# The T5 bias table laid out by the host and loaded in two pieces, and other dummy matmuls ahead of the first product

## The chip, the cores and the metric

One core of one Trainium2 chip runs the whole program. The metric is the device time of one execution in microseconds. The kernel before took 1897.99 us, the median of 3 runs (1896.04 to 1899.41).

## The reference, cut to what matters

Two transformer layers (`first_block`), then a layer with two other attentions and a product-key expert network (`second_block`), all in float32 for 256 tokens of width 1024. What the change touches is the bias of the sliding-window attention in the first two layers: a table of 32 buckets and 16 heads, spread over the distance between query and key. It is the same in both layers.

```
def sliding_window_attention(q, k, v, sinks, rel_bias):
    ...
    dist = np.arange(W)[:, None] + W - np.arange(2 * W)[None, :]
    bias = rel_bias.astype(jnp.float32)[t5_bucket(dist)]
    bias = bias.transpose(2, 0, 1).reshape(A_KV_HEADS, A_GROUP, W, 2 * W)
    valid_rel = jnp.asarray((dist >= 0) & (dist < W))
    ...
    logits = jnp.where(valid[None, :, None, None], scores + bias, -jnp.inf)
```

With W = 128, the table that the scores need has 128 queries x 16 heads x 256 keys: 2 MB in float32, with -1e30 outside the window.

## The kernel before, in words

**The products.** Nearly all of the work is matrix products of the activations with weights, each done as three float32r matmuls (`three`, lines 431 to 434; `prod_m`, lines 499 to 501), because a float32 operand is split into a high and a low part. The weights stream from HBM through the class `Weights`: `load` puts a block of 1 MB into one of three buffers (`raw`) from the SyncE queue, `first` makes the high part of half a block on ScalarE (line 264, six buffers `whi`), `second` the low part on VectorE (line 273, five buffers `wlo`). When both halves of a block are split, its buffer is free, and `second` issues the load of the block three further on. `pump` keeps the splitting four halves ahead of the half that is used. Blocks are numbered here from 0 in the order of `plan()`, halves likewise: block 8 is halves 16 and 17.

**The order.** `tc.manual_schedule()` keeps every engine's instructions in the order in which the Python code emits them, and every queue issues its DMAs in that order. Attention and other small work is woven between the products: generators stand in three lanes, and `tick()`, called at fixed places of a product, advances lane 0 or 1 at a rate, and lane 2 at `clock[4]`, which is 1.0 here, so one step of lane 2 for each tick. In `prod_t` with 8 input tiles each output block j has four ticks: after k = 3 and k = 7 of its first half, after k = 3 of its second, and at its end.

**The start.** The first block and the input come in pieces on the SyncE queue. Until they are there, five float32 matmuls on a tile of ones (`warm`, lines 356 and 357) keep TensorE at work. Their result is not used.

**The bias table.** `bias_load` (line 642) runs before the first layer: it takes the two tiles `BT[0]` and `BT[1]` (8 heads each, 1 MB each), loads the bucket table `rb` and the one-hot rows `oh`. `bias_table` (line 650) is put into lane 2 ahead of the product `aq` of layer 0 (line 791). It lets 15 ticks go by (`BW`), and at the 16th a matmul makes a row of 384 biases for each head (line 653), VectorE masks it (line 654), a DMA on GpSimd's queue writes 32 copies of it to DRAM (`toep`, line 658), and 8 more (line 663) read it back with a step of 383, so that each partition gets the row shifted by one.

**Who reads it.** `soft_pair` (line 699) does two heads. Its scores come from TensorE (lines 679 and 681), VectorE adds the bias of `BT[j // 4]` and takes the maximum (line 707), ScalarE the exponentials (line 714), VectorE scales them (lines 720 to 724), TensorE transposes them (line 729, six transposes for a pair), ScalarE copies them back (line 732), TensorE multiplies by the values (lines 690 and 692). In both layers the first pair's scores stand inside the first output block of the product `mqk`, the first six transposes follow the end of its second output block, then come four small transposes of the gates (lines 844 and 845), twelve product matmuls, and the next six transposes.

Of the kernel before, what the change touches and what calls it, by code (L numbers as in the profile page):

```python
# [9 lines left out]
F32 = mybir.dt.float32  # L10
F32R = mybir.dt.float32r
# [7 lines left out]
T = 256  # L19
KT = 8  # L20
EPS = 1e-6
NEG = -1e30
BW = 15
PR = (1.25, 1.65, 1.6, 1.5)
PZ = 2
GI = 3
LOOK, LAG, HI, LO, RAW = 4, 1, 6, 5, 3
FIRST, PIECE = 4, 512
NC = 32
NS, NA, NX, NB = 52, 60, 84, 96  # L30
KB = 0.61
GS = 2.0 ** 15
# [13 lines left out]
C_TRI = 256  # L46
C_CM = 384
C_ZM = 640
C_OH = 1024
C_ON = 1408  # L50
C_N = 1792

Q_HEADS = [(j, 4 + j) if j < 4 else (4 + j, 8 + j) for j in range(8)]

# [54 lines left out]
def lay_out(inp):  # L109

    f = {k: np.asarray(v) for k, v in inp.items()}
    offs = dict(mqk=0, mv=1024, mo=2048, gates=3072, aq=3080, ak=4104, av=4360, ga=4616, gb=5640)
    offs2 = dict(qa=0, ka=512, va=1024, qb=1536, kb=2048, vb=2560, g2a=3072, g2b=4096)
    hq = [h for pr in Q_HEADS for h in pr]
    aqcols = np.concatenate([np.arange(h * 64, h * 64 + 64) for h in hq])

    def tk(w, j):
        k = w.shape[0] // 128
        n = 16 // k
        b = w[:, j * n * 128:(j + 1) * n * 128].reshape(k, 128, n, 128)  # L120
        return b.transpose(1, 2, 0, 3).reshape(128, 2048)

    def mk(w, c0, nc, k0):
        nk = 2048 // nc
        b = w[k0 * 128:(k0 + nk) * 128, c0:c0 + nc].reshape(nk, 128, nc)
        return b.transpose(1, 0, 2).reshape(128, 2048)

    order = plan()
    wst = np.empty((len(order), 128, 2048), np.float32)
# [3 lines left out]
    for i, (nm, l, j) in enumerate(order):  # L133
        if nm == "aq":
            b = tk(waq[l], j)
        elif nm in ("ak", "mqk", "ga", "gb"):
            b = tk(f["w_in"][l][:, offs[nm]:offs[nm] + 1024], j)
        elif nm == "av":
            b = mk(f["w_in"][l], offs[nm], 256, 0)
        elif nm in ("mv", "mo"):  # L140
            b = mk(f["w_in"][l], offs[nm] + 512 * j[0], 512, 4 * j[1])
        elif nm == "ba":
            b = tk(wba[l], j)
        elif nm == "bm":
            b = tk(f["w_branch_m"][l], j)
        elif nm == "wo":
            b = tk(f["w_out"][l], j)
        elif nm == "up":
            b = tk(f["w_up"][l], j)
        elif nm == "dn":  # L150
            b = mk(f["w_down"][l], 0, 1024, 2 * j)
        elif nm in ("qa", "ka", "qb", "kb", "g2a", "g2b"):
            b = tk(f["w_in_2"][0][:, offs2[nm]:offs2[nm] + 1024], j)
        elif nm in ("va", "vb"):
            b = mk(f["w_in_2"][0], offs2[nm], 512, 4 * j)
        elif nm == "om":
            b = tk(f["w_out_moba_2"][0], j)
        elif nm == "os":
            b = tk(f["w_out_sb_2"][0], j)
        elif nm == "mix":  # L160
            b = tk(f["w_mix_out_2"][0], j)
        elif nm == "wq":
            b = tk(f["peer_w_q_2"][0], j)
        elif nm == "u":
            b = u[j * 256:(j + 1) * 256].reshape(2, 128, 8, 128).transpose(3, 0, 2, 1).reshape(128, 2048)
        elif nm == "v":
            b = v[j * 256:(j + 1) * 256].reshape(2, 128, 1024).transpose(1, 0, 2).reshape(128, 2048)
# [11 lines left out]
    for l in range(2):  # L179
# [9 lines left out]
    ii, jj = np.arange(128)[:, None], np.arange(128)[None, :]  # L189
    cst = np.zeros((128, C_N), np.float32)  # L190
    cst[:, C_ID:C_ID + 128] = np.eye(128)
# [3 lines left out]
    cst[:, C_ZM:C_ZM + 128] = strict  # L195
    cst[:, C_ZM + 256:C_ZM + 384] = strict
    cst[:, C_IO:C_IO + 128] = jj
    dist = 255 - np.arange(384)
    ok = (dist >= 0) & (dist < 128)
    n = np.maximum(dist, 0)  # L200
    large = 16 + (np.log(np.maximum(n, 1) / 16) / np.log(128 / 16) * 16).astype(np.int32)
    bucket = np.where(n < 16, n, np.minimum(large, 31))
    oh = (np.arange(32)[:, None] == bucket[None, :]) & ok[None, :]
    cst[:32, C_OH:C_OH + 384] = oh
    cst[:16, C_ON:C_ON + 384] = np.where(ok, 0.0, NEG)[None]

    q = np.arange(128)[:, None]
    c = np.arange(256)[None, :]
    dd = (128 + q - c).astype(np.float32)
    slopes = np.exp2(-np.arange(1, 9, dtype=np.float32))  # L210
    ali = np.where(dd >= 0, -slopes[:, None, None] * dd, np.float32(NEG)).astype(np.float32)
# [9 lines left out]
        "mg": np.ascontiguousarray(f["mlstm_norm_g"]),  # L221
        "fg": np.ascontiguousarray(f["final_norm_g_2"].reshape(1, D)),
        "sk": np.ascontiguousarray(f["peer_sub_keys_2"].reshape(16, 128, 128).transpose(2, 0, 1).reshape(128, 2048)),
        "rb": np.ascontiguousarray(f["rel_bias"][:, hq]),
    }


# [74 lines left out]
        return r  # L302


def body(tc, wst, xt, pk_d, cst_d, alibi_d, mg_d, fg_d, sk_d, rb_d, out):
    nc = tc.nc

    with tc.tile_pool(name="main", bufs=1) as sp, tc.tile_pool(name="wk", bufs=1) as wk, \
            tc.tile_pool(name="ws", bufs=1) as wp, tc.tile_pool(name="ps", bufs=1, space=PSUM) as ps, \
            tc.tile_pool(name="dr", bufs=1, space=bass.MemoryType.DRAM) as dr, tc.manual_schedule():  # L310
        pools = {}

        def slot(tag, dt=F32, n=2048):
            return pools["at"].tile([128, n], dt, name=tag, tag=tag)

        ws = Weights(nc, wp, wst, plan())
        mm, act, dve = nc.tensor.matmul, nc.scalar.activation, nc.vector

        def bank(tag, n):
            return ps.tile([128, 512], F32, name=tag, tag=tag, bufs=n)  # L320
# [7 lines left out]
        def sdb():  # L328
            return bank("sd", 1)

        def v3(t, a, b, off=0):
            return t[:, off:off + a * b].rearrange("p (a b) -> p a b", a=a)
# [13 lines left out]
        cst = wk.tile([128, 256], F32, name="cst")  # L346
# [6 lines left out]
        ones = wk.tile([128, 256], F32, name="ones")  # L353
        dve.memset(ones, 1.0)
        warm = sdb()
        for _ in range(5):
            mm(warm[:, :T], ones[:, :128], ones, start=True, stop=True)
        mhalf = wk.tile([128, 2], F32, name="mhalf")
        dve.memset(mhalf, -0.5)


        lanes = [deque(), deque(), deque()]
# [41 lines left out]
        def idle(n):  # L404
            for _ in range(n):
                yield
# [121 lines left out]
        def gain(i):  # L528
            return pk[:, PK_G + 8 * i:PK_G + 8 * i + 8]
# [20 lines left out]
        def norm_pair(j, g):  # L550
            for k in (2 * j, 2 * j + 1):
                act(H[0][:, k], X[:, k], AF.Identity, scale=g[:, k:k + 1])  # L552
            for k in (2 * j, 2 * j + 1):
                dve.scalar_tensor_tensor(H[1][:, k], X[:, k], g[:, k:k + 1], H[0][:, k].bitcast(F32),  # L554
                                         op0=OP.mult, op1=OP.subtract)
# [3 lines left out]
        def norm_sums(*later, now=True, ahead=LOOK):  # L559

            if ahead is not None:
                ws.pump(ws.used + 2 + ahead)
            later = list(later)
            if now:
                for _ in sum_sq(acc):
                    pass
            else:
                later[:0] = [(acc, None)]
            sums[:] = [sum_sq(a, g) for a, g in later]
            lanes[2].extend(sums)  # L570
# [68 lines left out]

        BT = []  # L640

        def bias_load():
            BT.extend(v3(slot(f"BT{i}"), 8, T) for i in range(2))
            rb = wk.tile([32, 16], F32, name="rb")
            nc.sync.dma_start(rb, rb_d)
            oh, row = [pools["at"].tile([128, 768], F32, name="oh", tag="L", bufs=2) for _ in range(2)]
            nc.sync.dma_start(oh, cst_d[:, C_OH:])
            return rb, oh, row[:16, :384]

        def bias_table(rb, oh, row):  # L650
            yield from idle(BW)
            p = sdb()
            mm(p[:16, :384], rb, oh[:32, :384], start=True, stop=True)
            dve.tensor_add(row, p[:16, :384], oh[:16, 384:])

            n = NC
            d = dr.tile([16, n, 384], F32, name="toep")
            nc.gpsimd.dma_start(d, row[:, None, :].to_broadcast([16, n, 384]))
            for i in range(2):
                for a in range(0, 128, n):  # L660
                    src = bass.AP(tensor=d.tensor, offset=d.offset + 8 * i * n * 384 + 127 - a,
                                  ap=[[383, n], [n * 384, 8], [1, 256]])
                    nc.gpsimd.dma_start(BT[i][a:a + n], src)
            yield


        OW = ((0, 128), (128, 256))
# [102 lines left out]
        def mixer(l):  # L770
# [11 lines left out]
                                             ap=[[0, 128], [1, D]]))  # L782
            wg = [pools["at"].tile([128, 160], F32R, name=n, tag="hm", bufs=2) for n in ("wgh", "wgl")]

            def ev_scaled(dst, r):
                def f(j, p):
                    dve.tensor_tensor(dst[:, 2 * j:2 * j + 2], v3(p, 2, T), b2(r), op=OP.mult)
                return f

            if l == 0:  # L790
                lanes[2].append(bias_table(*bias))
            prod_t("aq", H, ev_scaled(AQ, Rb8), 4, outer=(0,) if l else (), mid=mean_r if l else mean_0)
            parts(wg[0], wg[1], pk[:, PK_WG + 160 * l:PK_WG + 160 * l + 160])
            prod_t("ak", H, ev_scaled(AK, Rb), 1)
# [12 lines left out]
            for i in range(2):  # L807
                q = slice(32 * i, 32 * i + 4)
                dve.tensor_tensor(G[:, i], pg[q, :T], Rb[q], op=OP.mult)
                c = PK_BG + 2 * l + i  # L810
# [40 lines left out]
            c = PK_SK + 16 * l  # L851
# [575 lines left out]
        with tc.tile_pool(name="at", bufs=1) as pools["at"]:  # L1427
            ws.first()
            ws.second()
            for j in range(4):  # L1430
                norm_pair(j, gain(0))
            for _ in range(2):
                ws.first()
                ws.second()
            norm_sums(ahead=None)
            ws.pump(6)
            dve.tensor_mul(gff, gain(6), gain(4))
            bias = bias_load()
            pools["cst"] = pools["at"].tile([128, C_OH - 256], F32, name="catt")
            nc.sync.dma_start(pools["cst"], cst_d[:, 256:C_OH])  # L1440
            mixer(0)
            mlp(gain(2))
            mixer(1)
            acc2 = slot("BT1", n=512)
            mlp(gff, gain(6), acc2)
            mixer2(acc2)
# [23 lines left out]
```

## Time and profile before

| | |
|---|---|
| median of 3 runs | 1897.99 us |
| the profiled execution | 1896.21 us |
| its span, first to last instruction | 1894.4 us |
| mean granted clock of TensorE | 0.997 |
| DMA | 333.97 MB, 176 GB/s on the mean |

The profile is of one execution of its own, which lies 1.78 us under the median. 1.81 us of its time lie outside the span. Times in the rows are microseconds from the start of the span. A page of the profile gives totals; the views below are asked of the trace: who waited for whom, the instructions in order of time with the idle time ahead of each and what ended it, the chain of work that ended last, and sums by stretch.

### The profile page before, as it was taken

How to read it: one execution, taken by the hardware profiler on the slowest of the kernel's cores; microseconds unless marked ns; L12 is line 12 of the kernel's file. 1: busy time of each engine (PE TensorE's matmuls, PEld its weight loads, DVE VectorE, ACT ScalarE, POOL GpSimd, SP SyncE). 2: the span in 40 equal slices, each digit the busy share in tenths (PEclk: the TensorE clock that was granted, in tenths of full speed). 3: DMA queues.
4: the chain of work that ended last, by engine and by line, in shares of the span. 5: the costliest groups of instructions: out<-in, count | busy, mean ns of one | idle time of the engine just before them, and what ended most of it. 6: DMA issues, size and time to landing. Idle time of an engine off the chain costs nothing.

```text
span 1894.4 us, 34668 instructions
## 1 busy us (share of the span) xinstructions
PE 1878.1 (99%) x14450; PEld 1747.1 (92%) x14450; DVE 1351.8 (71%) x2426; ACT 977.5 (52%) x1441; POOL 28.0 (1%) x40
## 2 busy tenths in 40 slices
PE   9899999999999999999999999999999999999998
PEld 8779999999979999999989999999998888777786
DVE  5666666556686675556767799867988787888754
ACT  5476445445577455445555554644344444545443
POOL 0000000000000000000000000000000000000000
PEclk9999999999999999999999999999999999999999
DMA  8554445554344446454534545554445444555452
GB/s 287 166 178 145 160 181 206 182 196 165 148 161 163 156 179 222 178 184 162 189 134 162 217 163 197 191 185 156 157 159 188 167 179 178 200 189 178 165 194 87
DMA packets 48620, 333.97 MB, mean 176 GB/s; under 512 B 5656, under 2 KB 5920, under 8 KB 9552
## 3 DMA queue, kind: packets, MB, share of 16 engines
q1 hardware_dynamic: 46128, 322.29, 47.3%
q0 software_dynamic: 2048, 9.18, 1.8%
q8 instruction: 113, 1.85, 0.4%
q14 instruction: 43, 0.35, 0.1%
q10 hardware_dynamic: 288, 0.29, 0.0%
HBM read 328.85 MB, written 2.89 MB: 175 GB/s over the span
## 4 chain that ended last, share of the span: by engine, by line
PE 96%; DMA 2%; DVE 2%; ACT 0%; issue 0%; POOL 0%; SPq 0%; POOLq 0%; DVEq 0%; ACTq 0%
PE mm L432 17%; PE mm L433 17%; PE mm L434 17%; PE ac L1339 6%; PE ac L1341 6%; PE ac L1340 6%; PE ac L432 4%; PE ac L434 4%; PE ac L433 4%; PE mm L499 2%; PE mm L501 2%; PE mm L500 2%; PE sd L1277 1%; PE ac L1277 1%; PE ac L729 1%; PE ac L690 1%
## 5 line engine op out<-in xcount | busy, mean ns | idle before, releaser
L273 DVE TENSOR_TENSOR wlo<-raw,whi 128x1024 fp32r<-128x1024 f32 (+1 forms) x612 | 734.0, 1212 | 122.8 <-PE mm L434 61.9
L264 ACT CAST whi<-raw 128x1024 fp32r<-128x1024 f32 (+1 forms) x612 | 627.4, 1042 | 250.8 <-PE mm L433 128.6
L432 PE MATMUL mm<-Hh,whi 128*128 128x256 f32 x2288 | 654.7, 286 | 0.9 <-ACT Hh L552 0.9
L433 PE MATMUL mm<-Hl,whi 128*128 128x256 f32 x2288 | 645.0, 282 | 0.5 <-DVE Hl L554 0.3
L434 PE MATMUL mm<-Hh,wlo 128*128 128x256 f32 x2288 | 644.9, 282 | 0.2 <-DVE wlo L273 0.2
L432 PEld LDWEIGHTS mm<-Hh,whi 128*128 128x128 f32 x2288 | 431.7, 189 | 9.2 <-issue 5.8
L433 PEld LDWEIGHTS mm<-Hl,whi 128*128 128x128 f32 x2288 | 431.7, 189 | 1.7 <-DVE Hl L554 0.9
L434 PEld LDWEIGHTS mm<-Hh,wlo 128*128 128x128 f32 x2288 | 431.4, 189 | 0.4 <-DVE wlo L273 0.4
L1339 PE MATMUL ac<-whi,wvh 128*128 128x512 f32 x512 | 206.5, 403 | 0.0
L1341 PE MATMUL ac<-whi,wvl 128*128 128x512 f32 x512 | 202.9, 396 | 0.0
L1340 PE MATMUL ac<-wlo,wvh 128*128 128x512 f32 x512 | 201.9, 394 | 0.0
L432 PE MATMUL ac<-CV,whi 128*128 128x256 f32 x512 | 143.8, 281 | 0.0
L434 PE MATMUL ac<-CV,wlo 128*128 128x256 f32 x512 | 143.5, 280 | 0.0
L433 PE MATMUL ac<-MQ,whi 128*128 128x256 f32 x512 | 143.3, 280 | 0.0
L1341 PEld LDWEIGHTS ac<-whi,wvl 128*128 128x128 f32 x512 | 96.2, 188 | 22.8
L1340 PEld LDWEIGHTS ac<-wlo,wvh 128*128 128x128 f32 x512 | 96.5, 188 | 21.3
L1339 PEld LDWEIGHTS ac<-whi,wvh 128*128 128x128 f32 x512 | 96.4, 188 | 19.6
L1265 ACT COPY gs<-sd 128x252 f32<-128x252 f32 (+2 forms) x69 | 25.5, 370 | 153.1 <-PE sd L1277 153.1
L434 PEld LDWEIGHTS ac<-CV,wlo 128*128 128x128 f32 x512 | 96.7, 189 | 0.0
L433 PEld LDWEIGHTS ac<-MQ,whi 128*128 128x128 f32 x512 | 96.2, 188 | 0.0
L432 PEld LDWEIGHTS ac<-CV,whi 128*128 128x128 f32 x512 | 96.2, 188 | 0.0
L513 DVE TENSOR_TENSOR wvl<-A,wvh 128x512 fp32r<-128x512 f32 x58 | 40.0, 690 | 53.0 <-ACT wvh L512 47.7
(330 smaller groups left out, 2718.5 us busy)
## 6 DMA issues: line engine op xcount, KB each, us to landing
raw<-in_wst_dram SPq DMA_DIRECT2D x300, 1024.0 KB, 4.8
raw<-in_wst_dram SPq DMA_DIRECT2D x8, 512.0 KB, 7.7
BT<-toep POOLq DMA_DIRECT2D x8, 256.0 KB, 13.1
X<-in_xt_dram SPq DMA_DIRECT2D x4, 256.0 KB, 6.0
KV<-nMd POOLq DMA_DIRECT2D x2, 512.0 KB, 4.0
BT<-in_alibi_dram POOLq DMA_DIRECT2D x1, 1024.0 KB, 6.8
A<-in_sk_dram POOLq DMA_DIRECT2D x1, 1024.0 KB, 6.8
xs<-X POOLq DMA_DIRECT2D x1, 1024.0 KB, 10.1
```

What stands on the lines that cost most here:

```text
L264: self.nc.scalar.copy(hi[:, s], self.raw[p][:, h * 1024:(h + 1) * 1024][:, s])
L273: self.nc.vector.tensor_sub(lo[:, s], self.raw[p][:, h * 1024:(h + 1) * 1024][:, s], hi[:, s].bitcast(F32))
L432: mm(out_ap, hi, ah, start=first, stop=False, skip_group_check=True)
L433: mm(out_ap, hi, al, start=False, stop=False, skip_group_check=True)
L434: mm(out_ap, lo, ah, start=False, stop=last, skip_group_check=True)
L499: mm(o, a, hi[:, s], start=k == 0, stop=False)
L500: mm(o, a, lo[:, s], start=False, stop=False)
L501: mm(o, b, hi[:, s], start=False, stop=k == KT - 1)
L513: dve.tensor_sub(lo, src, hi.bitcast(F32))
L1339: mm(banks[i], a, hi, start=first, stop=False)
L1340: mm(banks[i], a, lo, start=False, stop=False)
L1341: mm(banks[i], c, hi, start=False, stop=last)
```

## The change

The host lays out the whole table (`bt`, 128 x 4096), and `bias_table` becomes two loads of 1 MB on the SyncE queue, straight into `BT[0]` and `BT[1]`: the first after 8 ticks of lane 2, the second after 4 more. `bias_load` goes, with its two loads, and with it go the matmul, the masking and the nine DMAs on GpSimd's queue. At the start four of the five float32 dummies stay, and nine float32r ones of 128, 64 and 96 columns follow, on a tile of ones that VectorE sets.

```diff
-BW = 15
+BW = 8, 4
...
+    bt = np.where(inside[:, :, None], f["rel_bias"][:, hq][bucket], np.float32(NEG)).transpose(0, 2, 1)
...
         warm = sdb()
-        for _ in range(5):
+        onesr = wk.tile([128, 512], F32R, name="onesr", tag="sq", bufs=2)[:, :128]
+        dve.memset(onesr.bitcast(F32), 1.0)
+        for _ in range(4):
             mm(warm[:, :T], ones[:, :128], ones, start=True, stop=True)
+        for n in (128, 128, 128, 64, 64, 64, 96, 96, 96):
+            mm(warm[:, :n], onesr, onesr[:, :n], start=True, stop=True)
...
-        def bias_load():
-            BT.extend(v3(slot(f"BT{i}"), 8, T) for i in range(2))
-            rb = wk.tile([32, 16], F32, name="rb")
-            nc.sync.dma_start(rb, rb_d)
-            oh, row = [pools["at"].tile([128, 768], F32, name="oh", tag="L", bufs=2) for _ in range(2)]
-            nc.sync.dma_start(oh, cst_d[:, C_OH:])
-            return rb, oh, row[:16, :384]
-
-        def bias_table(rb, oh, row):
-            yield from idle(BW)
-            p = sdb()
-            mm(p[:16, :384], rb, oh[:32, :384], start=True, stop=True)
-            dve.tensor_add(row, p[:16, :384], oh[:16, 384:])
-
-            n = NC
-            d = dr.tile([16, n, 384], F32, name="toep")
-            nc.gpsimd.dma_start(d, row[:, None, :].to_broadcast([16, n, 384]))
+        def bias_table():
+
             for i in range(2):
-                for a in range(0, 128, n):
-                    src = bass.AP(tensor=d.tensor, offset=d.offset + 8 * i * n * 384 + 127 - a,
-                                  ap=[[383, n], [n * 384, 8], [1, 256]])
-                    nc.gpsimd.dma_start(BT[i][a:a + n], src)
-            yield
+                yield from idle(BW[i])
+                nc.sync.dma_start(BT[i], bt_d[:, 2048 * i:2048 * i + 2048].rearrange("p (a b) -> p a b", a=8))
+                yield
...
-            bias = bias_load()
-            pools["cst"] = pools["at"].tile([128, C_OH - 256], F32, name="catt")
-            nc.sync.dma_start(pools["cst"], cst_d[:, 256:C_OH])
+            BT.extend(v3(slot(f"BT{i}"), 8, T) for i in range(2))
+            pools["cst"] = pools["at"].tile([128, C_N - 256], F32, name="catt")
+            nc.sync.dma_start(pools["cst"], cst_d[:, 256:])
```

## Rows read from the trace of the kernel before

**Rows 1.** The page: busy time, share of the span and instructions of each engine.

```profile
PE 1878.1 (99%) x14450; PEld 1747.1 (92%) x14450; DVE 1351.8 (71%) x2426; ACT 977.5 (52%) x1441; POOL 28.0 (1%) x40
```

**Rows 2.** Waits of TensorE, whole span: us in total, times, longest.

```profile
PE ac L729 <- DVE L L724: 4.5, 1, 4.5
...
PE mm L432 <- ACT Hh L552: 0.9, 1, 0.9
...
PE mm L434 <- DVE wlo L273: 0.2, 1, 0.2
```

**Rows 3.** The chain that ended last, 32 to 60 us: start, us, what.

```profile
34.51 9.55 DMA toep<-oh
...
46.14 12.00 DMA BT<-toep
```

**Rows 4.** Timeline of VectorE, layer 0: start, us, instruction, idle before and its releaser.

```profile
51.07 1.21 DVE L273 TENSOR_TENSOR wlo<-raw,whi 128x1024 fp32r<-128x1024 f32 x1
58.31 0.35 DVE L707 CUSTOM_DVE_ANT_0 L<-ac,BT,pk 128x128 f32<-128x128 f32 x1 [6.03 <-DMA BT<-toep]
...
66.81 1.03 DVE L724 TENSOR_TENSOR L<-L,sm 128x256 f32<-128x256 f32 x2
```

**Rows 5.** Timeline of TensorE, layer 0, first scores to the products after the transposes.

```profile
49.38 0.49 PE L679 MATMUL ac<-KV,AQ 64*128 64x128 f32 x4
...
62.65 0.28 PE L434 MATMUL mm<-Hh,wlo 128*128 128x256 f32 x1
67.38 0.30 PE L729 MATMUL ac<-cst,L 128*128 128x128 f32 x1 [4.45 <-DVE L L724]
67.98 1.30 PE L729 MATMUL ac<-cst,L 128*128 128x128 f32 x5 [0.30 <-DVE sm L720]
...
74.62 0.30 PE L432 MATMUL mm<-Hh,whi 128*128 128x256 f32 x1
```

**Rows 6.** Timeline of TensorE, the same places in layer 1.

```profile
491.29 0.49 PE L679 MATMUL ac<-KV,AQ 64*128 64x128 f32 x4
...
504.69 0.82 PE L729 MATMUL ac<-cst,L 128*128 128x128 f32 x6
...
508.39 0.28 PE L432 MATMUL mm<-Hh,whi 128*128 128x256 f32 x1
```

**Rows 7.** Timeline of VectorE, layer 1: the first pair's last step.

```profile
502.64 1.03 DVE L724 TENSOR_TENSOR L<-L,sm 128x256 f32<-128x256 f32 x2
```

**Rows 8.** Sums by stretch: busy us of each engine, granted clock, DMA share, GB/s.

```profile
66.00:70.00 4.00, 2.23 (x11) 1.67 (x11) 3.86 (x12) 1.19 (x3) 0.53 (x1) 0.73 0.41 171
70.00:75.00 5.00, 5.00 (x25) 5.00 (x25) 3.85 (x6) 3.08 (x7) 0.00 (x0) 0.54 0.60 213
...
504.00:508.00 4.00, 4.00 (x37) 3.81 (x35) 3.72 (x9) 0.63 (x3) 0.56 (x1) 1.00 0.11 17
```

**Rows 9.** Timeline of TensorE around the table's matmul of line 653.

```profile
32.59 0.28 PE L434 MATMUL ac<-Hh,wlo 128*128 128x256 f32 x1
...
33.54 0.39 PE L432 MATMUL mm<-Hh,whi 128*128 128x256 f32 x1
```

**Rows 10.** The SyncE queue: issues of weight blocks 5 to 7, 8 and 10.

```profile
21.37 8.22 SPq L241 DMA_DIRECT2D raw<-in_wst_dram  x3
36.22 0.33 SPq L241 DMA_DIRECT2D raw<-in_wst_dram  x1
...
50.83 0.33 SPq L241 DMA_DIRECT2D raw<-in_wst_dram  x1
```

**Rows 11.** Timeline of ScalarE: splits that waited for blocks 5, 6 and 8 to land.

```profile
29.55 2.00 ACT L264 CAST whi<-raw 128x1024 fp32r<-128x1024 f32 x2 [2.20 <-DMA raw<-in_wst_dram]
...
32.02 1.99 ACT L264 CAST whi<-raw 128x1024 fp32r<-128x1024 f32 x2 [0.25 <-DMA raw<-in_wst_dram]
...
47.82 1.05 ACT L264 CAST whi<-raw 128x1024 fp32r<-128x1024 f32 x1 [0.81 <-DMA raw<-in_wst_dram]
```

**Rows 12.** Timeline of TensorE: the dummy matmuls at the start.

```profile
1.19 4.63 PE L357 MATMUL sd<-ones 128*128 128x256 f32 x10 [1.19 <-DVE mhalf L359]
```

More of the change, by code (lines that the diff above doesn't have):

```diff
@@ L28 @@
 FIRST, PIECE = 4, 512
-NC = 32
 NS, NA, NX, NB = 52, 60, 84, 96
@@ L48 @@
 C_ZM = 640
-C_OH = 1024
-C_ON = 1408
-C_N = 1792
+C_N = 1024
 Q_HEADS = [(j, 4 + j) if j < 4 else (4 + j, 8 + j) for j in range(8)]
@@ L197, in lay_out @@
     cst[:, C_IO:C_IO + 128] = jj
-    dist = 255 - np.arange(384)
-    ok = (dist >= 0) & (dist < 128)
+    q = np.arange(128)[:, None]
+    c = np.arange(256)[None, :]
+    dist = 128 + q - c
     n = np.maximum(dist, 0)
@@ L202, in lay_out @@
     bucket = np.where(n < 16, n, np.minimum(large, 31))
[L203 to L208, printed above, removed]
+    inside = (dist >= 0) & (dist < 128)
+    bt = np.where(inside[:, :, None], f["rel_bias"][:, hq][bucket], np.float32(NEG)).transpose(0, 2, 1)
     dd = (128 + q - c).astype(np.float32)
@@ L223, in lay_out @@
         "sk": np.ascontiguousarray(f["peer_sub_keys_2"].reshape(16, 128, 128).transpose(2, 0, 1).reshape(128, 2048)),
-        "rb": np.ascontiguousarray(f["rel_bias"][:, hq]),
+        "bt": np.ascontiguousarray(bt.reshape(128, 4096)),
     }
@@ L302, in get_all, with body @@
         return r
-def body(tc, wst, xt, pk_d, cst_d, alibi_d, mg_d, fg_d, sk_d, rb_d, out):
+def body(tc, wst, xt, pk_d, cst_d, alibi_d, mg_d, fg_d, sk_d, bt_d, out):
     nc = tc.nc
@@ L790, in mixer @@
             if l == 0:
-                lanes[2].append(bias_table(*bias))
+                lanes[2].append(bias_table())
             prod_t("aq", H, ev_scaled(AQ, Rb8), 4, outer=(0,) if l else (), mid=mean_r if l else mean_0)
```

## The prediction

> **What bounds the kernel now.** The page comes first: TensorE is busy for 1878.1 us, 99% of the span [rows 1], so an edit counts only by what it takes from TensorE's stream or from TensorE's waits. The list of those waits comes second, because it is short: the longest is one wait of 4.5 us for VectorE's line 724, more than all the others together, and the next are 0.9 and 0.2 us at the start [rows 2]. So the third question is why line 724 was late. VectorE's timeline answers it: after the split that ends at 51.07 + 1.21 = 52.28 VectorE does nothing for 6.03 us, until the bias table has landed [rows 4]. The chain of waits shows where the table was: 9.55 us in the write to DRAM, then 12.00 us in the strided read back [rows 3]. Fourth, TensorE's timeline: it runs on with products until 62.65 + 0.28 = 62.93, then has nothing that it may do for 4.45 us, and once more for 0.30 us [rows 5]. Fifth, the sums by stretch: the granted clock is 0.73 of full in 66 to 70 us and 0.54 in 70 to 75 us [rows 8]. With two levels, 1 and 0.5, that is (1 - 0.73) / 0.5 x 4 + (1 - 0.54) / 0.5 x 5 = 2.16 + 4.60 = 6.76 us at 1.2 GHz, behind the idle stretch. So the table costs twice: once as idle time, once as a low clock after it.
>
> **What the stage would take with the table there.** This needs no model, since layer 1 runs the same code with the table long in place. From the first scores (line 679) to the fourth product behind the second six transposes (line 432) layer 0 takes 74.62 - 49.38 = 25.24 us [rows 5], layer 1 takes 508.39 - 491.29 = 17.10 us [rows 6]. The difference is 8.14 us. It splits as the views say it should: 4.45 + 0.30 = 4.75 us idle, and 3.39 us left, which is half of the 6.76 us at the low clock (3.38). In layer 1 the transposes follow the products at once, at 504.69, and the clock stays at 1.00 [rows 6, 8].
>
> **The change part by part.**
>
> *The table made by the host.* It removes TensorE's matmul of line 653. The product before it starts at 32.59 and lasts 0.28, the one behind it starts at 33.54 [rows 9]. Without the matmul the second would start between 32.59 (the whole step, 0.95 us, gone) and 32.87 (0.67 us gone); I take the middle, 0.81 us. This lies on the path, since TensorE has no wait there. The masking on VectorE and the nine DMAs of GpSimd's queue go too, at no gain of their own: nobody but the table waited for them.
>
> *The wait at line 707.* With the table there, VectorE goes on at 52.28 instead of 58.31. Its last step for the first pair, line 724, then ends at 66.81 + 1.03 - 6.03 = 61.81 [rows 4], ahead of the 62.93 at which TensorE wants it, by 1.12 us (the 0.81 us from above moves both). In layer 1 the same slack is 504.69 - (502.64 + 1.03) = 1.02 us [rows 6, 7]. So TensorE's wait goes as a whole, and I take the 8.14 us of layer 1. Next in line behind it is the split of weights on VectorE and ScalarE, which in layer 1 holds up nothing in this stretch.
>
> *The two loads.* Counting ticks: the ninth step of lane 2 comes in the third output block of `aq`, after the first four inputs. By then five halves have been asked for, `pump` has split eight, and blocks 0 to 6 are issued. The first load stands behind block 6 on the SyncE queue, the second, at the 14th tick, behind block 7 and ahead of block 8. Blocks 5 to 7 are issued between 21.37 and 29.59, block 8 at 36.22 [rows 10]. Blocks 5 and 6 land just ahead of the splits at 29.55 and 32.02 that waited for them, so a block of 1 MB takes 2.47 us when the queue is full [rows 11]. Then the first table lands by 32.0 + 2.5 = 34.5, block 7 by 37.0, the second table by 39.4, block 8 by 41.9. The first table is wanted at 52.28 - 0.81 = 51.5: a margin of 17 us. Block 7 is read by the second output block of `mqk`, 24 or 48 products before 62.93, so after 55; block 8 landed only about 47.8 before, with the table's DMAs beside it [rows 11], and comes earlier now. Both tiles are new, so neither issue has anything to wait for; an issue is 0.33 us of SyncE [rows 10]. The cost is nothing; the cover is that margin, and if it is gone each us late costs 1 us. The loads of `rb` and `oh`, 0.4 MB, go from the same queue.
>
> *The dummies.* Ten instructions take 4.63 us [rows 12], so the eight that stay take 3.70 and end at 4.89. For float32r matmuls of 64 to 128 columns no row exists. From below: 25 TensorE instructions at the low clock, nearly all products of 256 columns, take 5.00 us [rows 8], so 864 columns take at least 864 / 256 x 0.20 = 0.68 us. From above: at the float32 price, 0.93 us for 256 columns, 3.13 us. They end between 5.6 and 8.0. The first product is let go by ScalarE 0.9 us after 5.82, at 6.74 [rows 2, 12]. So they cost nothing, or push the first product by up to 1.3 us, of which the later wait of 0.2 us for a split [rows 2] gives some back: 0 to 1.1 us. A gain is bounded by the same waits, 0.9 + 0.2 = 1.1 us, but what ends those is a split or a landing and not TensorE. I take 0, because short float32r instructions are nearest to the products of 0.20 us.
>
> **The sum.** 8.14 + 0.81 = 8.95 us. From the profiled execution, 1896.21 (span 1894.4 and 1.81 outside it), this makes 1887.3. The median of the runs is 1.78 above that execution; no row says where those 1.78 us lie. If they lie in the table's DMAs or the clock behind them, they go, and if elsewhere they stay: 1887.3 or 1889.0. I take the middle, 1888.1.
>
> **The rivals.**
>
> *The clock falls at the transposes even without an idle stretch.* Then the 3.39 us stay, 5.56 go, and the time is 1888.1 + 3.4 = 1891.5. For it: the low stretch has both kinds of transposes in it [rows 5, 8]. Against it: the same sixteen in layer 1 ran at 1.00 [rows 6, 8]. The Trainium skill, page "TensorE: Matmul & The Clock Gate", section "Part 4: PE-mode transpose", says that a transpose does not count for the clock as other matmuls do; by that rule layer 1 would have slowed as well, and its trace disagrees. Chance 0.06.
>
> *The wait moves.* VectorE goes on at 51.5, but a split of weights in its stream waits for ScalarE or for a buffer that TensorE frees, and line 724 ends more than the 1.1 us later. With 2 us of idle time left and the clock falling behind it, 8.95 - 2 - 3.39 = 3.6 us are won: 1893.5. Layer 1 speaks against it, with the same number of splits between the scores and line 724. Chance 0.07.
>
> *The table is still late.* That the change does not do what it says would need the first load to stand behind block 10, issued at 50.83 [rows 10], instead of block 6, so that it lands about 58 as before: only the 0.81 us is won, 1897.2. My count of ticks would have to be off by four blocks. Chance 0.04.
>
> *Slower: SyncE stands at the table's load.* Every weight from block 7 on is queued behind the first load. If the tile's space is not free in the eyes of the scheduler, SyncE stands at that issue and no weight follows. Block 7 has some 18 us to spare (37 against 55), the change wins 9, so it decides from about 27 us of standing; 33 us would give 1894. For a stand of 40 us the time is 1888.1 + 40 - 18 = 1910. Against it: nothing writes or reads the two tiles before. Chance 0.03.
>
> **How the numbers follow.** The forecast has a chance of 0.80, with its own range of 1886 to 1890.5: from the lowest run, 1896.04 - 8.95 - 1.1 = 1886.0, to 1889.0 and the 1.1 us that the dummies may cost, with 0.4 for noise. The range that should hold the time reaches to the clock's rival and most of the moved wait: 1885.8 to 1893. A measurement of this kernel tells 0.2%, 3.8 us, from no change. Faster than 1894.2: the forecast, the clock's rival and over half of the moved wait, 0.90. Within 1894.2 to 1901.8: the late table and the rest, 0.07. Slower: 0.03.
>
> **What the profile after should show.** No wait for a table on VectorE; TensorE's first six transposes of layer 0 at 61.8 to 62.1, directly behind the product; a clock of 1.00 from 60 to 80 us; layer 1's first scores about 9 us earlier, at 482.3; blocks of weights around the table landing by 42; no wait of TensorE over 1 us after the start. A clock below 1 there shows the second case, a wait at line 729 the third, a wait for the table's DMA the fourth, ScalarE waiting for weights the last. The prediction is wrong in its size if layer 0's stage does not come out at layer 1's 17.1 us.

## The result, and the profile after

The changed kernel takes 1869.97 us, the median of four runs (1869.44 to 1870.33), against 1898.17 (1896.04 to 1899.41) for the kernel before beside it: a ratio of 0.9852 (95% interval 0.9835 to 0.9869). That is 28 us, where 9 were forecast, and below the range, which began at 1885.8. The profiled execution took 1869.44 us.

The stage on which the forecast rests came out as forecast. TensorE's timeline of the kernel after (start, us, instruction, idle time before it and what ended it), at the places of [rows 5]:

```profile
47.74 0.49 PE L661 MATMUL ac<-KV,AQ 64*128 64x128 f32 x4
...
59.30 0.28 PE L431 MATMUL mm<-Hh,whi 128*128 128x256 f32 x1
59.41 0.28 PE L432 MATMUL mm<-Hl,whi 128*128 128x256 f32 x1
...
60.55 0.28 PE L433 MATMUL mm<-Hh,wlo 128*128 128x256 f32 x1
60.66 0.82 PE L711 MATMUL ac<-cst,L 128*128 128x128 f32 x6
61.98 0.22 PE L827 MATMUL sd<-cst,ww 4*128 4x4 f32 x1 [0.35 <-DVE ww L821]
63.74 0.82 PE L711 MATMUL ac<-cst,L 128*128 128x128 f32 x6
...
64.76 0.28 PE L431 MATMUL mm<-Hh,whi 128*128 128x256 f32 x1
```

From the first scores to the fourth product behind the second six transposes: 64.76 - 47.74 = 17.02 us, against 25.24 before [rows 5] and 17.10 in layer 1 [rows 6]. The first six transposes follow their product at once. The waits of TensorE over the whole span, and then the sums over 62 to 70 us (length, busy us of PE, PEld, DVE, ACT and POOL with instructions, granted clock, DMA share, GB/s), show the same:

```profile
PE mm L431 <- ACT Hh L551: 1.2, 1, 1.2
PE sd L354 <- DVE ones L349: 1.2, 1, 1.2
PE sd L827 <- DVE ww L821: 0.8, 2, 0.5
PE mm L432 <- DVE MQ L512: 0.3, 1, 0.3
```

```profile
62.00:66.00 4.00, 4.00 (x35) 3.98 (x36) 3.76 (x6) 2.23 (x6) 0.00 (x0) 1.00 0.44 141
66.00:70.00 4.00, 4.00 (x36) 3.35 (x37) 2.58 (x4) 2.68 (x5) 0.00 (x0) 1.00 0.85 330
```

The 4.5 us of [rows 2] are gone and the clock is 1.00 where it was 0.73 [rows 8]. The two loads stand where the count of ticks put them, one behind blocks 5 and 6, one behind block 7 (the SyncE queue of after):

```profile
20.81 2.60 SPq L236 DMA_DIRECT2D raw<-in_wst_dram  x2
23.46 0.42 SPq L645 DMA_DIRECT2D BT<-in_bt_dram  x1
29.39 0.33 SPq L236 DMA_DIRECT2D raw<-in_wst_dram  x1
29.77 0.43 SPq L645 DMA_DIRECT2D BT<-in_bt_dram  x1
```

With 10.5 us from issue to landing (`BT<-in_bt_dram` in the page's list of DMA issues, the median of the two) they land at about 34 and 40, 17 us before VectorE adds the first bias.

But the stage is not where most of the time went. Matching the products of both traces one by one and subtracting their starts gives (start in before, difference in after):

| us in before | 52 | 80 | 307 | 508 | 708 | 908 | 1108 | 1309 | 1609 |
|---|---|---|---|---|---|---|---|---|---|
| after less before, us | -1.7 | -10.0 | -12.4 | -13.9 | -16.0 | -17.4 | -20.3 | -23.6 | -26.5 |

Ten us are won by 80 us, where all of the edit's work is done. Another 16.5 us come in steadily over 1500 us in which both kernels execute the same instructions. In the stretch above, the twelve products from 59.30 to 60.66 stand 1.36 / 12 = 113.3 ns apart (from start to start, called a step below); steps between products of the same form were 118.7 ns on the mean in before (steps over 135 ns are left out of the means here and below, unless it is said otherwise). Between 80 and 1609 us of before there are 7371 steps between two products that read `Hh` or `Hl`, of 127.4 ns on the mean before and 125.0 after (wider ones among them): 7371 x 2.4 ns = 17.5 us, which covers the 16.5. Nothing in the diff speaks of a product. One thing under the products did change: the 64 bytes per partition of the tile `rb` are gone from pool `wk`, and the weights' buffers `raw`, `whi` and `wlo`, allocated behind it, lie 64 bytes lower. (Most of the attention's tiles lie 6208 bytes lower, since `oh` is gone too; against the weights that is 6144, a multiple of 128.) In the addresses of the two built programs, in bytes per partition, `whi` went from 78336 to 78272 and `wlo` from 102912 to 102848, while `Hh` stayed at 28800 and `Hl` at 36992. The distance from `Hh` to `whi` was 49536, a multiple of 128; it is now 64 off.

### The profile page after: what moved, and what is told of

The parts are those of the page before. It is cut to its first block, busy times and chain, and to the rows that moved or that the text cites. A ratio compares the mean times of both kernels' runs of the same rounds, so it can differ in the third digit from the quotient of the medians.

```text
span 1867.7 us, 34657 instructions
## 1 busy us (share of the span) xinstructions
PE 1855.9 (99%) x14455; PEld 1729.0 (93%) x14455; DVE 1350.9 (72%) x2426; ACT 977.2 (52%) x1441; POOL 22.7 (1%) x31
## 4 chain that ended last, share of the span: by engine, by line
PE 96%; DVE 2%; ACT 0%; issue 0%; DMA 0%; POOLq 0%; POOL 0%; SPq 0%; DVEq 0%; ACTq 0%
PE mm L431 17%; PE mm L432 17%; PE mm L433 17%; PE ac L1321 7%; PE ac L1323 6%; PE ac L1322 6%; PE ac L431 4%; PE ac L433 4%; PE ac L432 4%; PE mm L498 2%; PE mm L500 2%; PE mm L499 2%; PE sd L1259 1%; PE ac L1259 1%; PE ac L672 1%; DVE wlo L268 1%
## 5 line engine op out<-in xcount | busy, mean ns | idle before, releaser
L1322 PEld LDWEIGHTS ac<-wlo,wvh 128*128 128x128 f32 x512 | 96.9, 189 | 20.3
## 6 DMA issues: line engine op xcount, KB each, us to landing
BT<-in_bt_dram SPq DMA_DIRECT2D x2, 1024.0 KB, 10.5
```

The source lines that it names most:

```text
L1322: mm(banks[i], a, lo, start=False, stop=False)
```

## The experiments

Two theories stood at first: **A**, the place of the weights in SBUF sets how fast one product follows another, and **B**, the start (the shorter dummies) sets it. Times below are medians with their ranges, the ratios are to the kernel before on the same chip.

**e1: after with 64 bytes put back.** This is the change as the prediction had costed it.

```diff
+        wk.tile([32, 16], F32, name="rb")
         def bias_table():
```

> The kernel after with one tile of 64 bytes a partition put where the table's small input stood, which nothing touches; it moves the weight buffers raw, whi and wlo up by 64 bytes, to where they lie in the kernel before, and changes no instruction. Theory A (place): 18 of the 28 us come from products that step faster because the weights lie 64 bytes lower against the activations; then this takes 1869.97 + 17 = 1887, and a product steps every 118.5 ns again. Theory B (start): the other dummy matmuls set TensorE off in a quicker rhythm that it keeps; then this stays at 1870, with steps of 113 to 117 ns.

Measured: 1885.33 us (1884.82 to 1885.82), ratio 0.9933 (0.9911 to 0.9956). The first and the last of 15 products in the middle of the expert's projections (timeline of TensorE, e1):

```profile
1119.81 0.28 PE L433 MATMUL mm<-Hh,wlo 128*128 128x256 f32 x1
...
1121.47 0.28 PE L432 MATMUL mm<-Hl,whi 128*128 128x256 f32 x1
```

1.66 us for 14 steps, 118.6 ns, as in before. Over 15 us are lost to a tile that nobody reads or writes.

**e2: after with the five old dummies**, without `onesr`.

```diff
-        for _ in range(4):
+        for _ in range(5):
             mm(warm[:, :T], ones[:, :128], ones, start=True, stop=True)
-        for n in (128, 128, 128, 64, 64, 64, 96, 96, 96):
-            mm(warm[:, :n], onesr, onesr[:, :n], start=True, stop=True)
```

> The kernel after with the five float32 dummies of the kernel before and no others; the weights lie as in the kernel after. Theory A (place of the weights): 1870, with steps of 113 to 117 ns. Theory B (start): 1887, with steps of 118.5 ns. If the time lies between, both have a part.

Measured: 1864.17 us (1861.36 and 1866.97), ratio 0.9822 (0.9786 to 0.9859), with the steps of after. The gain doesn't need the new dummies.

**e3: before with the new dummies alone** (the reverse of that edit).

> The kernel before with only the dummies of the kernel after; the bias table is made on the chip as before and the weights lie as before. Theory A (place of the weights): 1898, TensorE's wait of 4.5 us for line 724 as before. Theory B (start): 1898 - 17 = 1881.

Measured: 1895.03 us (1893.41 to 1898.05), ratio 0.9992 (0.9981 to 1.0003), and the wait for the table stays (TensorE's waits, e3):

```profile
PE ac L733 <- DVE L L728: 4.1, 1, 4.1
```

So B falls.

**e4: before with `rb` moved** into one of the `sq` buffers, so that the weights lie 64 bytes lower and nothing else is different.

```diff
-            rb = wk.tile([32, 16], F32, name="rb")
+            rb = wk.tile([128, 512], F32, name="rb", tag="sq", bufs=2)[:32, :16]
```

> The kernel before, with the small input of the table put into a buffer that exists anyway, so that the weight buffers lie 64 bytes lower, as in the kernel after; all instructions as before. Theory A (place of the weights): 1898 - 17 = 1881, with steps of 113 to 117 ns, and the wait of 4.5 us for line 724 stays. Theory B (start): 1898.

Measured: 1869.78 us (1869.46 and 1870.10), ratio 0.9852 (0.9823 to 0.9881). The whole 28 us, with nothing of the change. One of TensorE's waits and as many products at the same time in e4:

```profile
PE ac L729 <- DVE L L724: 3.5, 1, 3.5
```

```profile
1119.83 0.28 PE L434 MATMUL mm<-Hh,wlo 128*128 128x256 f32 x1
...
1121.41 0.28 PE L433 MATMUL mm<-Hl,whi 128*128 128x256 f32 x1
```

The table is still late; 14 steps take 1.58 us, 112.9 ns each. Set against after, e4 is some 7 us behind until 1108 us and makes that up later: its products step at 113 ns in a stretch (1108 to 1234 us) in which after's step at 118, as e2's do below, and the rest comes back towards the end. So e4 equals after in its total, not in its parts.

**e5 and e6: which tiles matter?** A1 says what TensorE reads (`whi`, `wlo`), A2 says `raw`, from which the splits read; then A3 says the distance between weights and activations, A4 the address of the weights alone. e5 leaves `raw` low and lifts `whi` and `wlo` back. e6 lifts `H` and all behind it by 64 bytes: the weights are at their old address, the distance is that of after.

```diff
+        wp.tile([32, 16], F32, name="gap")    e5: behind cst, ahead of whi and wlo
...
+        sp.tile([32, 16], F32, name="gap")    e6: ahead of H
```

> The kernel after with a tile of 64 bytes a partition, which nothing touches, behind the raw buffers: raw stays 64 bytes lower than in the kernel before, whi and wlo go back up to their old place. Theory A1 (what TensorE reads, whi and wlo, must lie off the old place): 1885, steps of 118.6 ns. Theory A2 (the place of raw, which the DMAs write and ScalarE and VectorE read, makes the difference): 1870, steps of 113 to 118 ns.

> The kernel after with 64 untouched bytes ahead of the activations Hh and Hl, which moves them and all that lies behind them up by 64 bytes: the weights lie where the kernel before has them, and the distance from activations to weights is that of the kernel after. Theory A3 (the distance counts): 1870, steps of 113 to 118 ns. Theory A4 (the place of the weights alone counts): 1885, steps of 118.6 ns.

Measured: e5 1884.28 us (1884.12 to 1884.79), ratio 0.9938 (0.9915 to 0.9960), as e1. e6 1865.29 us (1864.98 and 1865.60), ratio 0.9835 (0.9807 to 0.9864). What counts is what TensorE reads, and of that the distance between its two operands. That one of them lies on a multiple of 128 is not it either: in after `HA` and `whi` both lie 64 bytes off such a place, a multiple of 128 apart, and step at 118.9 ns on the mean. The sums of the same 20 us in e1 and in e6 show it as a count of products (columns as above; a matmul cut by an edge is counted too):

```profile
1120.00:1140.00 20.00, 20.00 (x171) 20.00 (x171) 20.00 (x88) 10.47 (x13) 0.00 (x0) 1.00 0.54 197
```

```profile
1120.00:1140.00 20.00, 20.00 (x178) 20.00 (x178) 20.00 (x86) 8.86 (x11) 0.00 (x0) 1.00 0.58 202
```

TensorE is busy throughout at a clock of 1.00 in both. The busy share, by which the kernel looked full, hides 4% here.

**e7: 32 bytes instead of 64** (the tile of e1, half as wide).

> The kernel after with 32 untouched bytes ahead of the weight buffers: they lie 32 bytes lower than in the kernel before instead of 64. If any distance off the old one lets the quicker rhythm come (steps of 113.3 or 117.7 ns): 1864 to 1872. If it takes 64 bytes: 1885, steps of 118.6 ns.

Measured: 1882.03 us (1881.66 and 1882.39), ratio 0.9924 (0.9895 to 0.9952); mean steps of 117.7 to 117.9 ns. Half the distance gives about 3 of the 15 us.

**e8: the attention's activations moved too.** `HA`, `HB`, `AQ`, `CV`, `KV` lie a multiple of 128 bytes from the weights in after; a tile of 64 bytes ahead of them in pool `at` ends that. `MQ`, which the expectation names with them, doesn't: it lies 32 bytes off such a distance in after and 32 off on the other side in e8.

> The kernel after with 64 untouched bytes ahead of the attention's tiles, so that the activations HA, HB, CV, AQ and MQ, which in both kernels lie at the same distance from the weights (a multiple of 128 bytes off each other), lie 64 bytes off it; Hh, Hl and the weights stay. Theory A3 (the distance counts): the products against these, some 2800 with steps of 117 to 119 ns, step at 113 to 118 too, and 1 to 13 us go: 1857 to 1869. Theory A4 (the place of the weights alone): 1870, their steps unchanged.

Measured: 1864.17 us (1861.77 and 1866.57), ratio 0.9829 (0.9798 to 0.9861). The mean steps of `HB` fall from 118.8 to 115.0 ns, of `HA` from 118.7 to 114.8, of `KV` from 118.8 to 115.3 and of `CV` with `whi` from 117.8 to 115.9, while those of `MQ` rise from 117.5 to 119.1 and of `CV` with `wlo` from 117.6 to 118.4. By 307 us this is worth 2.6 us against after. Of the 7.7 us at the end 4.7 come between 1108 and 1309 us, in products that e8 doesn't touch.

**e9 to e12: can the places be chosen for the best sum?** e9 lifts the weights by 128 bytes from after (distance again 64 off) and puts 64 bytes ahead of the `sq` buffers, which shifts the table `wvh` of the expert's last products; e10 adds the edit of e8, e11 the old dummies to that; e12 is after once more.

> The kernel after with 64 untouched bytes ahead of the buffers sq (which hold wvh in the expert products) and 64 more ahead of the weight buffers, so that whi and wlo lie 128 bytes higher than in the kernel after, and 64 bytes off their old distance to wvh. If the distance counts in steps of 128 bytes, the products against Hh and Hl step at 113 to 118 ns as in the kernel after, and the expert products of 512 columns against wvh and wvl, three of which take 700.5 ns in the kernel after, take 695.5 as in the kernel with the 64 bytes; 512 of each, so 2.6 us go: 1867. If it counts in longer steps, or by the place itself, the products step at 118.6 ns: 1882 to 1885.

> As the kernel with the weights 128 bytes up, and the attention's tiles another 64 bytes up, so that all activations lie 64 bytes off a multiple of 128 from the weights. Theory A3 (the distance counts): the products against HA, HB and the others quicken as in the run that moved the attention's tiles alone, 3 to 8 us: 1859 to 1864. Without it: as the kernel with the weights 128 bytes up.

> As the kernel with both moved, with the five float32 dummies of the kernel before. If the dummies matter only until the first products, which start 0.7 us earlier with the old ones: within 1 us of the kernel with both moved. If they set the rhythm of what follows: a difference of 3 us or more either way, seen in the stretches where the steps switch between 113.3 and 117.7 ns.

> The kernel after once more beside the three others: 1870, to tell whether they beat it.

Measured: e9 1872.58 us (1870.24 to 1873.37), e10 1875.47 (1873.25 to 1875.85), e11 1873.31 (1870.72 to 1875.25), e12 1868.60 (1864.32 to 1869.11). The edits that should have added up made it slower. The products with `Hh` and `Hl` still have the two steps of after, 113.3 and 117.8 ns, but fewer have the fast one: 35% of the steps are at most 114 ns in after, 24% in e9 and 9% in e10, where the mean is 117.4. The simple rule, fast when the distance is not a multiple of 128, is refuted as a rule. The expert's products of 512 columns did follow the distance from `whi` to `wvh`, as e9 expected: three steps take 695 ns in every kernel where it is 64 off (e1, e3, e5, e9 to e11) and 700 in every one where it is a multiple of 128 (after, e6, e8, e13).

**e13 to e16: what is left open, and the best version.** Several kernels had come out at one of two times some 5 us apart. e13 is after with the old dummies and every tile where after has it; e14 has the old dummies, no `onesr`, and the edit of e8; e15 and e16 are e2 and e8 again.

> The kernel after with the five float32 dummies of the kernel before, and every tile where the kernel after has it (the run with the old dummies had also moved the buffers sq, which hold wvh, by 96 bytes). If the dummies cost by themselves: 1864 to 1866, with the expert products of 512 columns as in the kernel after (700.5 ns for three). If the moved buffers were the gain: 1868 to 1870.

> The kernel after with the old dummies (buffers sq 96 bytes higher) and the attention's tiles 64 bytes up. If the two gains add, 5.8 + 5.8: 1858. If either depends on the rhythm that TensorE happens to fall into: 1860 to 1868.

> The kernel after with the old dummies once more, in more rounds: 1864, the median of the two earlier runs, if these were typical; 1867 to 1870 if the lower one was chance.

> The kernel after with the attention's tiles 64 bytes up once more, in more rounds: 1864, the median of the two earlier runs, if these were typical; 1866 to 1870 if the lower one was chance.

Measured: e13 1866.50 us (1863.94, 1864.10, 1868.90, 1869.10), e14 1861.85 (1859.10, 1859.39, 1864.32, 1864.46), e15 1861.94 (1861.86 to 1862.35), e16 1864.14 (1861.68, 1861.72, 1866.55, 1866.61). e14, ratio 0.9815 (0.9799 to 0.9832), and e15, 0.9820 (0.9804 to 0.9836), come out below both kernels (after: 0.9852, and 0.9842 in e12, whose interval reaches into theirs); their medians can't be told apart.

e2 and e15 are one kernel, profiled at 1866.97 and at 1862.35. Their traces agree within 0.7 us until 1107 us; between 1107 and 1307 the second gains 4.7. The same 20 us in e2, then in e15, and 120 us later in both:

```profile
1120.00:1140.00 20.00, 20.00 (x172) 20.00 (x171) 20.00 (x82) 8.81 (x10) 0.00 (x0) 1.00 0.60 212
...
1240.00:1260.00 20.00, 20.00 (x179) 20.00 (x178) 10.07 (x9) 9.70 (x12) 0.00 (x0) 1.00 0.66 231
```

```profile
1120.00:1140.00 20.00, 20.00 (x179) 20.00 (x178) 20.00 (x84) 9.59 (x12) 0.00 (x0) 1.00 0.59 211
...
1240.00:1260.00 20.00, 20.00 (x179) 20.00 (x178) 8.92 (x8) 9.25 (x11) 0.00 (x0) 1.00 0.54 192
```

So with the same addresses, the same instructions and the same clock TensorE held a step of 117.7 ns in one execution and of 113.3 in the other. But most stretches don't tip. In all ten profiles with `Hh` 64 off and the weights not at e9's place (after, e2, e4, e6, e8, e12 to e16) the products from 1275 to 1394 us of after have the slow step, those from 1235 to 1272 the fast one. One stretch of some 1090 products, 1104 to 1234 us of after, goes either way: slow in after, e2, e12, e13 and e14, fast in e4, e6, e8, e15 and e16. 1090 x 4.4 ns = 4.8 us, which is the distance of the two times. What tips it wasn't found: e13 and after share every address, and each has come out at both values. Between the profiles in which it is slow, the gains of e2 and e8 add up: e2 ends 2.5 us ahead of after, e8 without the stretch 2.9, e14 5.1.

## Why the prediction was right and wrong

Against its own kernel, the one whose products step as before (e1), the forecast can be read term by term:

| term | forecast | measured, e1 against before |
|---|---|---|
| the stage of layer 0 | -8.14 | -8.28 (-0.15 at 52 us, -8.43 from 80 us on) |
| the matmul of line 653 | -0.81 | -0.95 (+0.79 at 31 us, -0.16 at 35) |
| the dummies | 0 (0 to +1.1) | +0.79 (the start, 15 to 31 us; not shown to be theirs) |
| sum | -8.95 | -8.44 |
| the expert's last products | none | -2 (-8.71 at 1408 us, -10.55 at 1808) |

**The stage.** Right, and by the step that carried it: layer 1 is layer 0 with the table there. e1's timeline of TensorE gives 66.24 - 49.22 = 17.02 us:

```profile
49.22 0.49 PE L663 MATMUL ac<-KV,AQ 64*128 64x128 f32 x4
...
62.61 0.82 PE L713 MATMUL ac<-cst,L 128*128 128x128 f32 x6
...
66.24 0.28 PE L431 MATMUL mm<-Hh,whi 128*128 128x256 f32 x1
```

Its first transposes at 62.61 miss the forecast 61.8 to 62.1 because the forecast took all of the 0.81 off and e1's start gave 0.79 back. The same is true of layer 1's first scores: 482.73 in e1 where 482.3 was forecast, and 477.29 in after.

**The slack of VectorE** in layer 0 of after is smaller than the 1.12 us of the forecast:

```profile
59.22 1.03 DVE L706 TENSOR_TENSOR L<-L,sm 128x256 f32<-128x256 f32 x2
```

60.66 - 60.25 = 0.41 us (in e1, whose products step as before, it is 62.61 - 61.68 = 0.93): the products ahead of the transposes have become faster, VectorE has not. It still covers the transposes; what is late next is `ww` (line 827 of after), 0.35 us, which is why after's stage takes 17.02 us although its products step faster than e1's.

**The matmul of line 653** cost 0.95 us, the upper of the two bounds: the product behind it moved up by the whole step, not by the middle that was taken.

**The dummies.** Where the products settle, at 15 us, e1 is 0.79 us behind before and e3 0.64, inside the bounds given. That isn't shown to be the dummies' cost: after is 0.49 behind there and e12, the same kernel, 0.06; e2 with the old dummies 0.20 and e15, the same kernel, 0.90. In after the first product starts at 7.53, not at 6.75:

```profile
4.41 1.88 PE L356 MATMUL sd<-onesr 128*128 128x128 f32 x9
7.53 0.39 PE L431 MATMUL mm<-Hh,whi 128*128 128x256 f32 x1 [1.23 <-ACT Hh L551]
```

The dummies end at 6.29, between the 5.6 and 8.0 that were bounded; the product waits for ScalarE's split, as it did before, and that split waited 0.42 us for the input to land. Behind it the clock falls for a moment (sums over 9 to 13 us of after):

```profile
9.00:13.00 4.00, 4.00 (x23) 4.00 (x23) 3.25 (x8) 3.25 (x8) 0.00 (x0) 0.57 1.03 419
```

That is not the new dummies' doing, since e13 with the old ones has 0.62 there and e12, with the new ones, 1.00. And after and e13 stay within 0.35 us of each other throughout: at after's addresses the new dummies are worth nothing that these runs can tell.

**The rivals.** None came. The clock didn't fall at the transposes; the sixteen of layer 0 now run at 1.00 as well (62 to 70 us above, and 60 to 64 us in the same view). The Trainium skill, page "TensorE: Matmul & The Clock Gate", section "Part 4: PE-mode transpose", says that the full clock doesn't engage for transposes; this trace disagrees a second time, for groups of at most 0.82 us between products. The wait didn't move, the table wasn't late, and SyncE didn't stand. Two slips in the prediction bear on nothing else: by its own sum, 33 us of standing would give 1888.1 + 33 - 18 = 1903 and not 1894, and the list of TensorE's waits has more entries than it names behind the 4.5 us (1.2 ahead of the first dummy, 0.6 in two, twice 0.3).

**Where it was wrong.** The failed step is the sum, 8.14 + 0.81: it puts the change of every product's own step at nothing, and the text gives no reason for it, since it never asks whether what the diff doesn't name keeps its duration. The loss of `rb` was costed as a load that leaves the queue; that it was also 64 bytes of SBUF ahead of the weights was not asked. e1 against after prices that at 15.4 us, e4 against before at 28 (with the wait for the table still in it). It could not have been priced from the trace of before, where every product with `Hh` stands at one distance; but TensorE's stream is where all of the time passes [rows 1], and 2.4 ns on the mean of 7371 steps are worth more than everything that was in the sum. The rest of the difference, from e1's 1885.3 to the forecast 1888.1, is mostly the 2 us that e1 wins in the expert's last products. There `whi` and `wlo` are multiplied with `wvh`, and three steps take 699.6 ns in before, 700.0 in after, 695.0 in e1 (only steps over 260 ns left out). e3 has 695.0 too, and shares with e1 that `onesr` takes a `sq` buffer and so moves `wvh`.

## What to carry to other kernels

Where one engine runs back to back for the whole span, compare the mean step between equal instructions in both traces before any wait is credited with a gain: a share of 99% busy says nothing on how fast the stream goes. An edit that adds or drops a tile moves all tiles behind it; to measure the edit itself, hold the addresses with a tile of the same size, and to look for more, try such tiles by themselves. Gains from addresses need not add up (they did in e14 and didn't in e10), so each combination has to be run.

## What the runs showed of the hardware

Float32r products of 256 columns that read `Hh` or `Hl`, with a load of weights for each, follow each other at 118.6 or 118.7 ns on the mean when their two operands in SBUF lie a multiple of 128 bytes apart, and at 113.3 or 117.8 ns when they lie 64 bytes off that; 32 bytes off gave 117.7 to 117.9 (e7). The other activations show it less cleanly: at a multiple of 128 their means run from 117.5 (`CV`) to 122.9 (`AQ` with `wlo`, 32 products), at 64 off from 113.0 to 118.6. All of it is at a granted clock of 1.00 with TensorE busy without a gap. In the second case TensorE keeps one of the two steps for up to 170 us in after and 390 in e10. In the ten profiles above a place of the program mostly has the same one each time; one stretch of some 1090 products takes either in the same kernel, which makes runs 5 us apart. Three things stay open: what picks one of the two, and with it why e9 to e11 have fewer of the fast ones; why `CV` with `wlo` goes the other way in e8; and by which distance the products of 512 columns go beyond the two clear cases (64 off 695 ns for three steps, a multiple of 128 700), since e7, with `wvh` as far from `whi` as in e2 (32 bytes off a multiple of 128), takes 699.4 ns and e2 696.1. Whether two reads of SBUF meet in one place, which such a pattern suggests, is only argued: no row of the profile shows a read.
